# A Hymba layer on one core: the parts of the output weights are made at other turns and pinned on ScalarE

## The chip, the cores and the metric

The kernel runs on one core of one Trainium2 chip. The metric is the device time of one execution in microseconds; the median of three runs stands for a kernel. All data are float32. A core has five engines that run their own instruction streams and wait for each other by semaphores: TensorE (PE, with PEld for its weight loads), VectorE (DVE), ScalarE (ACT), GpSimd (POOL) and SyncE (SP), which here only issues transfers (DMA).

## The reference, cut to what matters

One decoder layer over 2048 tokens of width 1024. Half of the mixer is gated linear attention (GLA) with 4 heads in chunks of 64 tokens, half is dilated sliding-window attention with 8 heads and three (window, dilation) patterns. Both halves are put side by side and multiplied by W_out (1024 x 1024); the MLP follows.

```python
def reference(...):
    n = rmsnorm(x, attn_norm_g)
    # one projection W_in gives q, k, v, gates for GLA and q, k, v for attention
    mixed = concat([gla_mixer(...) * gate, combined dilated branches])
    h = x + mixed @ w_out
    h = h + square(relu(rmsnorm(h, mlp_norm_g) @ w_ff1)) @ w_ff2
    return rmsnorm(h, final_norm_g)
```

## The kernel before

The kernel runs in four stages. The input projection comes first. Then, up to about 880 us, attention and GLA run interleaved. The output projection (h = x + mixed @ W_out) goes to about 1080 us, and the MLP fills the rest.

Every large product works on numbers split in two: a high part, made by an ACT Copy to the type fp32r, and a low part, made by a DVE subtraction of the high part from the float32 value. Three matmuls, at L64, L65 and L66, then make one product (high by high, high by low, low by high). The split values of the mixer are `mT`: transposes at L393, the high part at L368 on ACT, the low part at L369 on DVE. The split values of W_out are `wo`, in eight blocks of 128 rows. For each, `load_wo` takes a buffer `woraw`, loads 512 KB into it (L985, issued by SP), makes the high part (L986, ACT) and the low part (L987, DVE). The projection of the first tokens needs all eight blocks.

Attention is cut into units of two or four blocks of 128 queries of one head and branch. A unit has three steps. `scores` makes the scores with two matmuls each (L744, L746) into the PSUM bank `ps_c`; DVE adds the bias and takes the row maximum (L756), and ACT takes the exponential into `pe` (L757). `transpose` transposes `pe` on PE (L766) into `ps_d`, and the result is copied to `pt` by ACT (L773) and DVE (L775) in turn. `values` multiplies `pt` by v (L785) into `ps_a`, and DVE copies that to O (L788). In turn k of the main loop stand the values of unit k - 2, the transposes of unit k and the scores of unit k + 3. There are four buffers each of `pe` and `pt`.

The GLA of 16 tiles of 128 tokens runs along, one step of a generator in most turns. Its instructions for tile t: the decay (matmul L912; exponentials L913 and L914 on ACT; products L915, L918 and L920 on POOL), the scores (matmul L925, masked copy L926 on DVE), the outputs (matmuls L945 and L946, copy L947, squares L949), the keys (transposes L955, copy L956), the output scale (the gate on POOL at L962, the scale on ACT at L964, and later the store to `mixD` at L862), and the state (matmul L970, DVE addition L973, ACT scale L975). The gates of the next tile but one are loaded to `sr` (L905), the values to `gv` (L904).

The branches of attention are combined on POOL and, for the last pair of heads, on DVE (the lines around L822 to L845).

What sets the order: the main loop records the instructions turn by turn, with a table `plan` of calls that a turn makes first (`at_unit`). From there a scheduler orders each engine's instructions by its own estimate of when they can start; `tc.keep_in_program_order(x)` pins x behind the instruction recorded just before it on its engine. SP issues its transfers strictly in its order, so a transfer that waits for its data holds up all those behind it. The eight calls of `load_wo` stand at turns NU - 28 + 3i for i = 0 to 7, so the last is 7 turns ahead of the end of the units. The load of x and of the mixer's tiles (`mx`, L1157) for the output projection follows behind all this, and the projection's first transposes (L393) are ordered into the last turns of attention.

Of the kernel before, what the change touches and what calls it, by code (L numbers as in the profile page):

```python
# [10 lines left out]
F32 = mybir.dt.float32  # L11
FR = mybir.dt.float32r
I32 = mybir.dt.int32
AF = mybir.ActivationFunctionType
OP = mybir.AluOpType
# [3 lines left out]
D = 1024  # L19
# [11 lines left out]
AHEAD, LAG = 3, 2  # L31
# [7 lines left out]
def emit(tc, a, stop=99):  # L39
    nc = tc.nc  # L40
    V, A, G, T, SP = nc.vector, nc.scalar, nc.gpsimd, nc.tensor, nc.sync
# [6 lines left out]
    def ps(tag):  # L48
        return psum.tile([128, 512], F32, name="ps_" + tag, tag=tag, bufs=BANKS[tag])

    def slot(name, dt=F32, n=SLOT):

        return up.tile([128, SLOT], dt, name=name, tag="u", bufs=25)[:, :n]

    def view(t, shape):
        n = int(np.prod(shape))
        names = "abcd"[:len(shape)]
        return t[:, :n].rearrange(f"p ({' '.join(names)}) -> p {' '.join(names)}", **dict(zip(names, shape)))
# [9 lines left out]
    def token_rows(ap, c, row, width=D):  # L68

        return bass.AP(tensor=ap.tensor, offset=ap.offset + c * 128 * row,  # L70
                       ap=[[row, 16], [16 * row, 8], [1, width]])
# [23 lines left out]
    def rstd_of(ssq, width, n=1, bias=eps):  # L95
        r = stat(n)
        A.activation(r, ssq, AF.Ln, bias=bias, scale=1.0 / width)
        A.activation(r, r, AF.Exp, scale=-0.5)
        return r
# [754 lines left out]
    def issue_later(n, *args):  # L854

        due.append((clock[0] + n, args))
# [37 lines left out]
    def gla_load(t):  # L894
        if t < NT:
            tk = slice(t * 128, t * 128 + 128)
            SP.dma_start(gst["g"][t % 2], glD[tk])
            SP.dma_start(gst["gq"][t % 2], gqD.rearrange("j p s -> p j s")[:, :, tk])
            SP.dma_start(gst["gk"][t % 2], gkD.rearrange("j p s -> p j s")[:, :, tk])

    def gla_load_v(t):
        if t < NT:
            tk = slice(t * 128, t * 128 + 128)
            SP.dma_start(gst["gv"][t % 2], gvD[tk])  # L904
            SP.dma_start(gst["sr"][t % 2], srD[tk])  # L905

    def gla_decay(t):

        g, ep, em = gst["g"][t % 2], gst["ep"][t % 2], gst["em"][t % 2]
        pb = view(ps("o"), (2, 256))  # L910
        for j in range(2):
            T.matmul(pb[:, j, :130], g[:, j * 128:j * 128 + 128], gst["rT"], start=True, stop=True)  # L912
        A.activation(ep, pb[:, :, :130], AF.Exp)  # L913
        A.activation(em, pb[:, :, :128], AF.Exp, scale=-1.0)  # L914
        G.tensor_tensor(em, em, gst["gk"][t % 2], op=OP.mult)  # L915
        for s in range(2):
            r = slice(64 * s, 64 * s + 64)
            G.tensor_tensor(gst["eq"][t % 2][r, :, s], ep[r, :, :128], gst["gq"][t % 2][r], op=OP.mult)  # L918
        if t:
            G.tensor_tensor(gst["w"][t % 2], gst["ep"][1 - t % 2][:, :, 129], ep[:, :, 128], op=OP.mult)  # L920

    def gla_scores(t):
        em, pa = gst["em"][t % 2], view(ps("o"), (4, 128))
        for j in range(2):
            T.matmul(pa[:, 2 * j:2 * j + 2], em[:, j], gst["eq"][t % 2][:, j], start=True, stop=True)  # L925
        V.copy_predicated(gst["AT"], gst["cm"][:, None, :].to_broadcast([128, 4, 128]), pa)  # L926

    def gla_steps():

        gla_decay(0)  # L930
        yield
        gla_scores(0)
        yield
        for t in range(NT):
            more = t + 1 < NT
            if more:
                gla_decay(t + 1)
                yield
            st, at, eq, em = gst["SS"], gst["AT"], gst["eq"][t % 2], gst["em"][t % 2]
            gv, sr, o, ss = gst["gv"][t % 2], gst["sr"][t % 2], gst["o"][t % 2], gst["ss"][t % 2]  # L940
            po = view(ps("o"), (2, 256))
            for j in range(2):
                for s in range(2):
                    h, oh = 2 * j + s, po[:, j, s * 128:s * 128 + 128]
                    T.matmul(oh, eq[:, j, s], st[:, j], start=True, stop=False)  # L945
                    T.matmul(oh, at[:, h], gv[:, h * 128:h * 128 + 128], start=False, stop=True)  # L946
            A.activation(o.rearrange("p (j s) e -> p j (s e)", s=2), po, AF.Copy)  # L947
            for h in range(4):
                A.activation(gst["sq"], o[:, h], AF.Square, accum_out=ss[:, h:h + 1])  # L949
            yield  # L950
            if more:
                kn = gst["kn"]
                pk = view(ps("o"), (2, 128))
                for j in range(2):
                    T.transpose(pk[:, j], em[:, j], ident)  # L955
                A.activation(kn, pk, AF.Copy)  # L956
                gla_load(t + 2)
                gla_load_v(t + 1)
                yield
                gla_scores(t + 1)  # L960
            rr = rstd_of(ss, 128, 4)
            G.tensor_tensor(o, o, view(sr, (4, 128)), op=OP.mult)  # L962
            for h in range(4):
                A.activation(o[:, h], o[:, h], AF.Copy, scale=rr[:, h:h + 1])  # L964
            issue_later(6, token_rows(mixD, t, D, width=512), o.rearrange("p h e -> p (h e)"))
            yield
            if more:
                pi, w = view(ps("o"), (2, 256)), gst["w"][1 - t % 2]
                for j in range(2):
                    T.matmul(pi[:, j], kn[:, j], gv[:, j * 256:j * 256 + 256], start=True, stop=True)  # L970
                for s in range(2):
                    r = slice(64 * s, 64 * s + 64)
                    V.tensor_tensor(st[r], st[r], pi[r, :, s * 128:s * 128 + 128], op=OP.add)  # L973
                for j in range(2):
                    A.activation(st[:, j], st[:, j], AF.Copy, scale=w[:, j:j + 1])  # L975
                yield

    wo = a["w_out"].rearrange("o (c p) n -> p (o c) n", p=128)
    WO = []

    def load_wo(n):
        for c in range(len(WO), len(WO) + n):
            raw = slot("woraw")[:, :D]
            w = view(slot("wo", FR), (2, D))
            SP.dma_start(raw, wo[:, c])  # L985
            A.activation(w[:, 0], raw, AF.Copy)  # L986
            V.tensor_tensor(w[:, 1], raw, w[:, 0].bitcast(F32), op=OP.subtract)  # L987
            WO.append(w)

    list(heads)  # L990
    for part in range(4):
# [32 lines left out]
    def at_unit(n, *f):  # L1024
        plan.setdefault(n, []).append(f)
# [45 lines left out]
    NU = len(units)  # L1071
    for i in range(8):
        at_unit(NU - 28 + 3 * i + AHEAD, load_wo, 1)
    gla = gla_steps()
    for k in range(-AHEAD, NU + LAG):
        tr, pv, sc = iter(()), iter(()), iter(())
# [354 lines left out]
    for at in range(7, len(jobs1)):  # L1431
# [13 lines left out]
        if at in (len(jobs1) - 4, len(jobs1) - 2):  # L1445
            n = (at + 4 - len(jobs1)) // 2
# [5 lines left out]
    for ph, (j, half) in enumerate(phases):  # L1452
        P = [bank() for _ in range(4)]
        for k in range(8):
            n = 8 * ph + k
# [53 lines left out]
def build(nc, inputs, stop=99):  # L1509
    arrays, aps = {}, {}  # L1510
    for name in _INS:
        arrays[name] = np.ascontiguousarray(inputs[name])
    arrays.update(_constants())
    for name, v in arrays.items():
        aps[name] = nc.dram_tensor(name, v.shape, mybir.dt.from_np(v.dtype), kind="ExternalInput").ap()
    aps["out"] = nc.dram_tensor("out", (1, S, D), F32, kind="ExternalOutput").ap()
    with tile.TileContext(nc, schedule_with_timeline_sim=True) as tc:
        emit(tc, aps, stop)
    return arrays
# [10 lines left out]
```

## Time and profile before

| what | us |
|---|---|
| median of 3 runs | 2313.16 (2312.07 to 2315.47) |
| the profiled execution | 2312.57 |
| its span | 2310.8 |
| PE busy | 2282.6 |
| DVE busy | 1550.3 |
| ACT busy | 1179.3 |
| POOL busy | 307.7 |

The mean granted clock of PE was 0.995 over the span. The page cuts the span in forty slices; attention and GLA end in slice 16 of them, where the output projection starts.

How to read it: a row of a view of waits names the instruction that waited and the one that released it, then the time in total, how often, and the longest. A row of a timeline gives the start in us from the span's start, the duration, the engine (SPq is SP's queue), the line, the operation, and the tiles out<-in; a run of like instructions is one row with its count, and in brackets stands the idle time before it, with what ended it. Rows of one engine overlap a little at their ends, so the distance of two starts is the time that an instruction holds its engine.

### The profile page before, as it was taken

How to read it: one execution, taken by the hardware profiler on the slowest of the kernel's cores; microseconds unless marked ns; L12 is line 12 of the kernel's file. 1: busy time of each engine (PE TensorE's matmuls, PEld its weight loads, DVE VectorE, ACT ScalarE, POOL GpSimd, SP SyncE). 2: the span in 40 equal slices, each digit the busy share in tenths (PEclk: the TensorE clock that was granted, in tenths of full speed). 3: DMA queues.
4: the chain of work that ended last, by engine and by line, in shares of the span. 5: the costliest groups of instructions: out<-in, count | busy, mean ns of one | idle time of the engine just before them, and what ended most of it. 6: DMA issues, size and time to landing. Idle time of an engine off the chain costs nothing.

```text
span 2310.8 us, 34890 instructions
## 1 busy us (share of the span) xinstructions
PE 2282.6 (99%) x12652; PEld 1975.6 (85%) x12652; DVE 1550.3 (67%) x2863; ACT 1179.3 (51%) x2368; POOL 307.7 (13%) x394
## 2 busy tenths in 40 slices
PE   8999999999999999999999999999999999999998
PEld 7977998799999998888888888888888888888887
DVE  8887778766667676346877788777755346447444
ACT  5574546435877873235555566555543323225224
POOL 1120002025385672000000000000000100000002
PEclk9999999999999999999999999999999999999999
DMA  4457854786668864678644447444486477447553
GB/s 165 144 183 230 250 161 125 215 254 229 209 203 249 253 218 143 210 244 279 208 153 151 151 163 265 151 151 150 150 278 238 155 280 251 148 166 279 188 170 109
DMA packets 341805, 457.59 MB, mean 198 GB/s; under 512 B 18118, under 2 KB 214231, under 8 KB 336257
## 3 DMA queue, kind: packets, MB, share of 16 engines
q1 hardware_dynamic: 336878, 446.71, 59.3%
q10 hardware_dynamic: 4754, 8.66, 1.0%
q8 instruction: 99, 1.62, 0.3%
q14 instruction: 74, 0.60, 0.1%
HBM read 292.99 MB, written 167.02 MB: 199 GB/s over the span
## 4 chain that ended last, share of the span: by engine, by line
PE 51%; ACT 1%; DMA 0%; DVE 0%; issue 0%; DVEq 0%; ACTq 0%
PE ps_c L64 6%; PE ps_c L65 6%; PE ps_c L66 6%; PE ps_a L65 4%; PE ps_a L66 4%; PE ps_d L65 4%; PE ps_d L64 4%; PE ps_a L64 4%; PE ps_d L66 4%; PE ps_o L65 2%; PE ps_o L66 2%; PE ps_o L64 2%; DMA w1raw<-w_ff 0%; ACT scr L1355 0%; DVE hb L369 0%; ACT hb L368 0%
## 5 line engine op out<-in xcount | busy, mean ns | idle before, releaser
L369 DVE TENSOR_TENSOR ca<-ra,ca 128x1024 fp32r<-128x1024 f32 x112 | 138.0, 1233 | 161.6 <-ACT ca L368 161.6
L368 ACT ACTIVATE ca<-ra 128x1024 fp32r<-128x1024 f32 x112 | 118.0, 1053 | 221.3 <-PE ps_c L66 184.3
L368 ACT ACTIVATE w1comb<-w1raw 128x512 fp32r<-128x512 f32 x224 | 140.0, 627 | 153.7 <-PE ps_c L66 55.7
L1357 POOL TENSOR_TENSOR suma<-suma,gs 128x512 f32<-128x512 f32 x16 | 23.4, 1475 | 1393.7 <-ACT scr L1355 1393.7
L369 DVE TENSOR_TENSOR w1comb<-w1raw,w1comb 128x512 fp32r<-128x512 f32 x224 | 153.9, 689 | 51.8 <-ACT w1comb L368 51.7
L785 PE MATMUL ps_a<-v,pt 128*128 128x65 f32 x1200 | 178.2, 252 | 2.5 <-ACT pt L773 1.8
L785 PEld LDWEIGHTS ps_a<-v,pt 128*128 128x128 f32 x1200 | 175.1, 195 | 3.5 <-ACT pt L773 2.1
L757 ACT ACTIVATE pe<-pe,O 128x256 f32<-128x256 f32 (+1 forms) x384 | 156.6, 453 | 39.4 <-DVE O L756 36.1
L766 PE MATMUL ps_d<-ident,pe 128*128 128x128 f32 x600 | 159.9, 279 | 0.0
L756 DVE CUSTOM_DVE_ANT_0 pe<-ps_c,nb 128x256 f32<-128x256 f32 (+1 forms) x384 | 126.9, 361 | 39.6 <-PE ps_d L766 18.4
L207 ACT ACTIVATE wcomb<-wraw 128x512 fp32r<-128x512 f32 (+2 forms) x126 | 97.2, 773 | 88.7 <-PE ps_o L65 22.6
L368 ACT ACTIVATE cb<-rb 128x1024 fp32r<-128x1024 f32 x56 | 59.4, 1060 | 159.3 <-PE ps_o L65 98.8
L66 PE MATMUL ps_c<-cb,ca 128*128 128x512 f32 x336 | 130.7, 389 | 0.0
L66 PE MATMUL ps_c<-hb,w1comb 128*128 128x512 f32 x336 | 130.7, 389 | 0.0
L65 PE MATMUL ps_c<-cb,ca 128*128 128x512 f32 x336 | 130.7, 389 | 0.0
L64 PE MATMUL ps_c<-hb,w1comb 128*128 128x512 f32 x336 | 130.7, 389 | 0.0
L65 PE MATMUL ps_c<-hb,w1comb 128*128 128x512 f32 x336 | 130.7, 389 | 0.0
L64 PE MATMUL ps_c<-cb,ca 128*128 128x512 f32 x336 | 130.7, 389 | 0.0
L766 PEld LDWEIGHTS ps_d<-ident,pe 128*128 128x128 f32 x600 | 110.1, 187 | 0.1
L369 DVE TENSOR_TENSOR cb<-rb,cb 128x1024 fp32r<-128x1024 f32 x56 | 68.3, 1222 | 62.0 <-ACT cb L368 62.0
L1219 ACT ACTIVATE acc<-acc 128x512 f32<-128x512 f32 x128 | 79.6, 631 | 51.5 <-DVE acc L1239 35.8
L64 PE MATMUL ps_a<-wo,mT 128*128 128x512 f32 x256 | 101.3, 396 | 0.0
(419 smaller groups left out, 7038.9 us busy)
## 6 DMA issues: line engine op xcount, KB each, us to landing
ra<-actD SPq DMA_DIRECT2D x56, 1024.0 KB, 6.9
actD<-acc SPq DMA_DIRECT2D x192, 256.0 KB, 2.3
rb<-w_ff SPq DMA_DIRECT2D x72, 512.0 KB, 4.8
w1raw<-w_ff SPq DMA_DIRECT2D x32, 1024.0 KB, 6.2
k<-kD SPq DMA_DIRECT2D x16, 1024.0 KB, 7.9
rb<-hTD SPq DMA_DIRECT2D x13, 1024.0 KB, 7.1
wraw<-w_in SPq DMA_DIRECT2D x48, 256.0 KB, 3.7
cmb<-boD SPq DMA_DIRECT2D x16, 528.0 KB, 7.0
```

The lines of the kernel that those rows point to most:

```text
L64: T.matmul(out, sh, mh, start=first, stop=False)
L65: T.matmul(out, sl, mh, start=False, stop=False)
L66: T.matmul(out, sh, ml, start=False, stop=last)
L207: A.activation(hi, src, AF.Copy, scale=sc)
L368: A.activation(hi, src, AF.Copy)
L369: V.tensor_tensor(lo, src, hi.bitcast(F32), op=OP.subtract)
L756: V.tensor_tensor_reduce(p, s, bias, scale=1.0, scalar=BIG, op0=OP.add, op1=OP.min, accum_out=nm)
L757: A.activation(p, p, AF.Exp, bias=nm, scale=-1.0)
L766: T.transpose(pb[:, i * 128:i * 128 + 128], src, ident)
L785: T.matmul(self.b.opsum[:, n % 4], self.pt[:, i * 128:i * 128 + 128], self.b.v[:, blk, cols], start=first, stop=last)
L1219: A.activation(v, v, AF.Relu)
L1357: G.tensor_tensor(C[0], C[0], gF[:, :512], op=OP.mult)
```

## The change

`load_wo` only loads and puts the buffer on a list. A new function, `split_wo`, takes the oldest buffer and makes both parts. For blocks 0 to 5 it is called in the turn of the load, right behind it; for blocks 6 and 7 two turns later. All eight ACT copies are pinned behind the instruction recorded just before them on ACT. No instruction is added or removed, and the buffers are taken in the same order.

```diff
+    raw_wo = []
+
     def load_wo(n):
-        for c in range(len(WO), len(WO) + n):
+        for c in range(len(WO) + len(raw_wo), len(WO) + len(raw_wo) + n):
             raw = slot("woraw")[:, :D]
-            w = view(slot("wo", FR), (2, D))
             SP.dma_start(raw, wo[:, c])
-            A.activation(w[:, 0], raw, AF.Copy)
-            V.tensor_tensor(w[:, 1], raw, w[:, 0].bitcast(F32), op=OP.subtract)
-            WO.append(w)
+            raw_wo.append(raw)
+
+    def split_wo():
+        raw, w = raw_wo.pop(0), view(slot("wo", FR), (2, D))
+        tc.keep_in_program_order(A.activation(w[:, 0], raw, AF.Copy))
+        V.tensor_tensor(w[:, 1], raw, w[:, 0].bitcast(F32), op=OP.subtract)
+        WO.append(w)
...
     for i in range(8):
         at_unit(NU - 28 + 3 * i + AHEAD, load_wo, 1)
+        at_unit(NU - 28 + 3 * i + (2 if i > 5 else 0) + AHEAD, split_wo)
```

The lines behind it move by 5 or 6: the load is L986 in the changed kernel, the high part L991, the low part L992, and the loads of `mx` L1163; the GLA and the units keep their lines. The order of instructions differs on every engine, between the third block's copy and the first tiles of the output projection.

The first place is ACT at the third and fourth block (counted from one). `O_9415` is the output of the last head pair's branch (128, 1), with which attention ends: a softmax into `pe` that names it belongs to the last units. Before:

```order
L956 ACTIVATE gla<-ps_o 128x256
L986 ACTIVATE wo<-woraw 128x1024
L98 ACTIVATE stats<-stats 128x4
L986 ACTIVATE wo<-woraw 128x1024
L773 ACTIVATE pt<-ps_d 128x512
L757 ACTIVATE pe<-pe,O_9415 128x128
L757 ACTIVATE pe<-pe,O_9415 128x256 x3
```

The same place of ACT in the changed kernel:

```order
L956 ACTIVATE gla<-ps_o 128x256
L98 ACTIVATE stats<-stats 128x4
L773 ACTIVATE pt<-ps_d 128x512
L975 ACTIVATE gla<-gla 128x128 x2
L964 ACTIVATE gla<-gla,stats 128x128 x4
L913 ACTIVATE gla<-ps_o 128x260
L914 ACTIVATE gla<-ps_o 128x256
L991 ACTIVATE wo<-woraw 128x1024 x2
L757 ACTIVATE pe<-pe,O_9415 128x128
L757 ACTIVATE pe<-pe,O_9415 128x256 x3
```

The two copies have moved behind the state, the output scale and the next decay of the recurrence (L975, L964, L913, L914), and these have moved ahead of the softmaxes of `O_9415`.

PE at the same place, before, from the masked scores of the recurrence on:

```order
L925 MATMUL ps_o<-gla 128x256 x2
L744 MATMUL ps_c<-k_8676,qs 128x256
L746 MATMUL ps_c<-k_8785,qs 128x256
L744 MATMUL ps_c<-k_8676,qs 128x256
L746 MATMUL ps_c<-k_8785,qs 128x256
L785 MATMUL ps_a<-v,pt 128x65 x4
L766 MATMUL ps_d<-ident,pe 128x128
```

And in the changed kernel, from the values ahead of the same masked scores on; three more pairs of L945 and L946 and the scores of `ps_c` follow, and then the first transpose (L766) of the last units:

```order
L785 MATMUL ps_a<-v,pt 128x65 x4
L925 MATMUL ps_o<-gla 128x256 x2
L785 MATMUL ps_a<-v,pt 128x65 x4
L970 MATMUL ps_o<-gla 128x256 x2
L912 MATMUL ps_o<-gla 128x130 x2
L945 MATMUL ps_o<-gla 128x128
L946 MATMUL ps_o<-gla 128x128
```

The state (L970), the decay (L912) and the outputs of the next tile (L945, L946) stand ahead of that transpose now; before they came behind some units of it.

SP at the end of attention, before, with the last two blocks' loads:

```order
L810 DMA cmb<-boD_1_103 128x8x132
L985 DMA woraw<-w_out 128x1024 x2
L1157 DMA mx<-mixD 128x512
L1157 DMA mx<-mixD 128x384
L862 DMA mixD<-gla 16x8x512
```

In the changed kernel:

```order
L810 DMA cmb<-boD_1_103 128x8x132
L986 DMA woraw<-w_out 128x1024
L862 DMA mixD<-gla 16x8x512
L986 DMA woraw<-w_out 128x1024
L1163 DMA mx<-mixD 128x512
L1163 DMA mx<-mixD 128x384
```

The last block's load stands behind the store of a GLA tile now. On ACT both of the last copies (L991 x2) stand directly ahead of the first high part of `mT` (L368), where before they were eight and four rows ahead of it, among the last softmaxes.

## The prediction

> **What bounds the kernel now.** I read the page first: the span and the busy time of the engines.
>
> ```profile
> span 2310.8 us, 34890 instructions
> PE 2282.6 (99%) x12652; PEld 1975.6 (85%) x12652; DVE 1550.3 (67%) x2863; ACT 1179.3 (51%) x2368; POOL 307.7 (13%) x394
> ```
>
> PE sets the end, so the change is worth what it adds to or takes from PE's idle time, or from its clock. The two programs stand in the same order on every engine except between about 836 and 895 us. There I asked for PE's waits (780 to 1100 us):
>
> ```profile
> PE ps_o L925 <- POOL gla L915: 1.9, 1, 1.9
> PE ps_a L785 <- ACT pt L773: 1.8, 1, 1.8
> PE ps_a L785 <- DVE pt L775: 0.7, 1, 0.7
> ```
>
> Three waits in two places. The windows of 2 us show what each drags behind it (columns: busy time of PE, PEld, DVE, ACT, POOL; granted PE clock; DMA share; GB/s):
>
> ```profile
> 840.00:842.00 2.00, 1.70 (x7) 1.54 (x8) 2.00 (x8) 2.00 (x7) 2.00 (x3) 0.77 0.00 0
> 842.00:844.00 2.00, 2.00 (x13) 2.00 (x11) 2.00 (x4) 0.25 (x1) 2.00 (x2) 0.50 0.76 221
> 844.00:846.00 2.00, 2.00 (x18) 2.00 (x18) 1.25 (x8) 0.82 (x2) 2.00 (x2) 0.87 0.93 303
> ...
> 870.00:872.00 2.00, 1.29 (x13) 1.10 (x12) 2.00 (x9) 1.88 (x5) 1.24 (x1) 0.95 0.84 268
> 872.00:874.00 2.00, 2.00 (x11) 2.00 (x12) 1.99 (x5) 1.05 (x3) 0.00 (x0) 0.50 0.97 276
> 874.00:876.00 2.00, 2.00 (x16) 2.00 (x16) 1.94 (x7) 1.29 (x3) 0.00 (x0) 0.69 0.94 363
> ```
>
> After each wait the clock falls to 0.50 for some 3.4 us. The clock's part is 2 us times what is missing to 1: 2 x (0.23 + 0.50 + 0.13) = 1.72 at the first place, 2 x (0.05 + 0.50 + 0.31) = 1.72 at the second. So place one costs 1.90 + 1.72 = 3.6 us, place two 1.84 + 0.70 + 1.72 = 4.3. More than 7.9 us is not to be won here.
>
> **The change, part by part.** No instruction is added or taken out: the same eight loads, ScalarE copies (L986) and VectorE subtractions (L987) stand elsewhere, and with them the recurrence (GLA) of the last tiles.
>
> *Place two goes: -4.3.* There ACT waits for block 7's load, copies block 8 next, and the pt copy that PE needs stands behind both:
>
> ```profile
> 865.30 1.06 ACT L986 ACTIVATE wo<-woraw 128x1024 fp32r<-128x1024 f32 x1 [1.99 <-DMA woraw<-w_out]
> 866.26 0.49 ACT L757 ACTIVATE pe<-pe,O 128x256 f32<-128x256 f32 x1
> ...
> 868.23 1.04 ACT L986 ACTIVATE wo<-woraw 128x1024 fp32r<-128x1024 f32 x1
> 869.17 0.57 ACT L773 ACTIVATE pt<-ps_d 128x512 f32<-128x512 f32 x1
> ```
>
> In the new order both copies stand behind the last of these pt copies, so nothing PE needs for attention waits for them. I credit all of it. What becomes late instead is the output projection (below).
>
> *Place one grows: +4.5.* Blocks 3 and 4 were copied at 835.9 and 838.5, ahead of the softmaxes (L757) of the last head's next units. Now their two copies stand together behind the recurrence: ACT holds L964, L913, L914, the two copies, and only then those L757, for which PE's transposes (L766) wait. POOL feeds L964, in an order that the change leaves alone up to there:
>
> ```profile
> 835.74 1.28 POOL L845 TENSOR_TENSOR O<-O,cmb 128x512 f32<-128x512 f32 x1
> 836.98 2.31 POOL L918 TENSOR_TENSOR gla<-gla 64x256 f32<-64x256 f32 x2
> 839.37 0.20 POOL L920 TENSOR_TENSOR gla<-gla 128x2 f32<-128x2 f32 x1
> 839.52 0.73 POOL L915 TENSOR_TENSOR gla<-gla 128x256 f32<-128x256 f32 x1
> 840.20 4.75 POOL L845 TENSOR_TENSOR O<-O,cmb 128x512 f32<-128x512 f32 x3
> 844.91 1.28 POOL L962 TENSOR_TENSOR gla<-gla 128x512 f32<-128x512 f32 x1
> ```
>
> POOL has no gap, so L962 again ends at 846.2. Its slowest forms may quicken when DVE is idler:
>
> ```profile
> 808.50 1.44 POOL L918 TENSOR_TENSOR gla<-gla 64x256 f32<-64x256 f32 x2 [1.27 <-ACT gla L913]
> ```
>
> That saves 0.9 us in L918; if the last of the L845, which take 1.6 us each, come near the 1.28 of the first, another 0.8 goes: 844.5 is the earliest. Then the loads. SP issues block 4's load behind the load of the next sr tile (L905), which waits for that same L962:
>
> ```profile
> 846.22 0.33 SPq L905 DMA_DIRECT2D gla<-srD  x1
> 846.67 0.36 SPq L985 DMA_DIRECT2D woraw<-w_out  x1
> ...
> DMA to landing us min/median/max: 4.3/5.2/6.0
> ```
>
> (The last line is that of the woraw tile.) So block 4 lands at 846.67 + 4.3 = 850.97 or, with the quicker POOL, at 849.3. Its copy takes 0.96 from start to start, the first L757 0.40, and the first L766 can begin at 850.7 to 852.4. Before it PE has, from 838.4 on, only eight L785 printed in two groups, L925, L970, L912, L945 with L946 and two scores:
>
> ```profile
> 847.45 1.03 PE L970 MATMUL ps_o<-gla 128*128 128x256 f32 x4
> 848.13 0.47 PE L744 MATMUL ps_c<-k,qs 128*128 128x256 f32 x1
> ...
> 850.89 0.61 PE L912 MATMUL ps_o<-gla 128*128 128x130 f32 x4
> 851.25 0.36 PE L744 MATMUL ps_c<-k,qs 128*128 128x256 f32 x1
> ...
> 879.22 1.00 PE L785 MATMUL ps_a<-v,pt 128*128 128x65 f32 x8
> ```
>
> By starts that is 0.68 for L970 and as much for L925, 0.36 for L912, about 1.8 for L785, some 1.8 for L945 and L946 (eight row pairs at 0.22), 0.5 for the scores: 5.7 us. From 838.4 to 850.7..852.4 are 12.3 to 14.0 us, so PE loses 6.6 to 8.3 there, idle time and slow clock together, against 3.6 before: +3.0 to +4.7. A second slow stretch of the clock after the restart would add to it. I take +4.5, near the upper end, since POOL's order is unchanged and DVE stays busy. VectorE's L926 and L973 and the low parts stand in this chain too, but end under the wait for the load. Below nothing it could come only if L962 ended by 841.5, which the POOL rows don't allow.
>
> *ACT is late afterwards: +1.9.* The held-up softmaxes make a queue on ACT.
>
> ```profile
> 846.20:857.40 11.20, 11.20 (x106) 11.10 (x106) 10.04 (x30) 10.36 (x26) 5.60 (x6) 1.00 0.92 279
> 857.40:871.50 14.10, 11.97 (x108) 11.29 (x107) 11.38 (x38) 11.77 (x36) 9.79 (x17) 1.00 0.85 254
> L757 ACT ACTIVATE pe<-pe,O 128x256 f32<-128x256 f32 x42 | 19.5, 500 | 2.8 <-DVE O L756 2.7
> ```
>
> ACT was busy 22.1 us of these 25.3 and PE 23.2: ACT can hardly catch up. Pricing the instructions of the new order by their starts here (L757 0.40, L773 0.47, L964 0.30, a block's copy 0.96), ACT has 20.4 us from the first tile's output after the hold-up (L947) to the pt copies of the last units, PE 17.7 up to the values that read them. The lag is between 0 (ACT ahead by its four pe buffers) and 2.6; I take 1.9, nearer the rows than the cover.
>
> *The output projection begins late: +4.8.* Block 8's load is now queued on SP behind the store of the last recurrence tile (L862), which waits for ACT's L964; before, blocks 7 and 8 were issued together ahead of it:
>
> ```profile
> 858.59 2.21 SPq L985 DMA_DIRECT2D woraw<-w_out  x2
> ...
> 867.99 0.52 SPq L862 DMA_DIRECT2D mixD<-gla  x1
> ```
>
> Call T the end of that L964. The load is issued at about T + 0.6 and lands 4.3 to 6.0 later. Block 8's copy stands on ACT ahead of the high parts of mT (L368), its low part on DVE ahead of the low parts (L369):
>
> ```profile
> L987 DVE TENSOR_TENSOR wo<-woraw,wo 128x1024 fp32r<-128x1024 f32 x8 | 11.6, 1445 | 3.0 <-DMA mx<-mixD 1.7 <-ACT wo L986 1.4
> 871.49 0.57 ACT L368 ACTIVATE mT<-ps_c 128x512 fp32r<-128x512 f32 x1
> 882.06 0.68 DVE L369 TENSOR_TENSOR mT<-ps_c,mT 128x512 fp32r<-128x512 f32 x1
> ```
>
> Copy 0.96, low part 1.45, mT 0.57 and 0.68, with 0.3 between them, is 4.0: the first projection matmul (L64) comes at T + 8.9 to T + 10.6. PE's attention work ends at about T + 4.3, and it has 1.9 us besides (transposes L393, a GLA output). PE idles 2.7 to 4.4 us less what the lag above already covers; I take 3.1, and a slow stretch of 1.7 as after both waits above: +4.8. It is nothing if ACT's last softmaxes are so late that block 8 has landed; at most 6.1.
>
> Sum: 4.5 - 4.3 + 1.9 + 4.8 = +6.9. The profiled execution took 2312.57 us, 0.6 under the median of 2313.16: 2312.57 + 6.9 = 2319.5, and by the median 2320.1. I say 2320.
>
> The page "TensorE: Matmul & The Clock Gate" of the Trainium skill (in "HAM oscillation — how this bites in real kernels") makes an abstract rule of "no PE-idle gaps >~3.4µs". The trace differs: 1.90 us of idle already brought 0.50. By the page the old waits would have cost their idle time alone, so that 2.5 is won at place two, 4.7 to 6.4 lost at place one (6.6 to 8.3 less 1.9), and the end costs 3.1: with the lag some 8 us instead of 6.9, an estimate, with the same sign.
>
> **The rivals.**
>
> *Both stalls vanish, faster.* The recurrence comes early and block 4's load lands before ACT gets there; 2312.57 - 7.9 = 2305 at best, 2308 if half of place one stays. For it: the two places are all that PE loses, and the order takes both copies out from before the softmaxes. It decides when L962 ends before 841.5, or SP lets block 4's load go ahead of L905. Against it stand the POOL rows. Chance 0.14.
>
> *The end is covered, no change.* Block 8 lands while the last softmaxes run: L64 starts on time, the lag hides there too, and only place one against place two is left: 2312.57 + 3.0..4.7 - 4.3, with a lag of 0 to 1.5: 2311 to 2315, say 2313. For it: 857 to 871 us gives ACT most of the time, so T and the end of attention may lie farther apart than 4.3. Chance 0.22.
>
> *Place two does not go either.* DVE, busy 21.4 us of the 25.3 above, gets the low parts, the softmax maxima and the combine in one bunch after the hold-up, and the pt copies on DVE (L775) come as late as the 0.70 of before, or worse: the 4.3 credited come back, less what the lag counts twice, 2322 to 2327. Chance 0.14, within slower. That the change fails to do what it says is part of this: parts two turns behind their loads still wait for the load if SP holds that back as well, as it does for block 8.
>
> **How the numbers follow.** My forecast, by its sum: 0.50, with its own range of 2315 to 2325 (place one 3.0, no lag and the end's idle at 2.7 with its clock below; all upper ends above). About 0.2% (4.6 us) is what a measurement of this kernel can tell from no change: under 2308.5 and over 2317.8. Of the forecast's 0.50 nearly all lies over 2317.8, with the third rival 0.64 in all; no change 0.22; faster 0.14. The range that leaves out 2 in 10 reaches from 2311, the low end of the covered case, to 2326.
>
> **What would show it.** Right: a wait of PE of 3 to 6 us at L766 (for ACT's L757) near 845 to 852, ACT's copy L991 before it waiting for woraw, clock 0.50 after it; no wait of L785 near 870; then a wait of L64 or L393 on block 8 or mT near 885 to 895. Wrong: block 4 landing before 846, L962 ending long before 846, PE's transposes running through 840 to 850, or no idle time ahead of the first L64. Then the sum loses 4.5 or 4.8 and the first or the second rival holds.

## The result, and the profile after

The changed kernel takes 2325.1 us in the median of 6 runs (2323.69 to 2326.99), the kernel before 2312.68 us (2312.07 to 2315.47, 6 runs): 12.4 us slower, ratio 1.0050 with a 95% interval of 1.0037 to 1.0063. The profiled execution of the changed kernel took 2325.71 us, its span is 2323.9 us, 13.1 more than before.

The waits of PE from 780 to 1120 us in the changed kernel, those of 0.7 us or more, stand here where the kernel before had the three rows of the prediction:

```profile
PE ps_d L393 <- POOL O L845: 3.4, 1, 3.4
PE ps_a L64 <- DVE O L788: 2.4, 1, 2.4
PE ps_o L945 <- ACT gla L914: 2.0, 1, 2.0
PE ps_d L766 <- ACT pe L757: 1.8, 1, 1.8
PE ps_a L785 <- DVE pt L775: 1.4, 1, 1.4
PE ps_o L912 <- PE ps_o L970: 1.0, 1, 1.0
PE ps_c L744 <- DVE O L756: 1.0, 1, 1.0
PE ps_a L785 <- ACT pt L773: 0.7, 1, 0.7
```

Three windows cut the stretch into place one, place two and the end of attention. The first number behind the length is PE's busy time, the one behind the five engines PE's granted clock. Before:

```profile
836.00:858.00 22.00, 20.10 (x170) 19.64 (x170) 19.26 (x58) 16.61 (x38) 15.65 (x15) 0.92 0.77 243
858.00:880.00 22.00, 19.45 (x166) 18.77 (x165) 19.27 (x61) 16.49 (x48) 12.29 (x24) 0.92 0.86 275
880.00:898.00 18.00, 18.00 (x94) 15.16 (x93) 14.07 (x31) 6.12 (x19) 8.36 (x10) 1.00 0.22 68
```

And in the changed kernel:

```profile
836.00:858.00 22.00, 16.02 (x117) 14.64 (x116) 12.54 (x38) 11.71 (x30) 13.65 (x15) 0.92 0.62 205
858.00:880.00 22.00, 21.29 (x199) 20.77 (x198) 17.35 (x68) 19.51 (x59) 4.17 (x11) 1.00 0.56 151
880.00:898.00 18.00, 10.52 (x54) 8.46 (x53) 17.81 (x31) 4.19 (x8) 17.53 (x24) 0.81 0.59 220
```

Idle time is the length less PE's busy time, the clock's part the length times what is missing to 1. Place one: 5.98 us idle against 1.90, with the same clock, +4.1. Place two: 0.71 against 2.55, and 1.76 of slow clock gone, -3.6. The end: 7.48 against none, and 3.4 of slow clock, +10.9. Together +11.4 of the 13.1. Where the other 1.7 us lie is not shown. Such sums hold to a few us: the span less these losses is 2302.8 us before and 2304.6 here, and lies between 2298.8 (e6) and 2306.2 (e12) in the profiled executions of all the runs below.

Place one follows the chain that was drawn. ACT in the changed kernel:

```profile
844.30 1.28 ACT L964 ACTIVATE gla<-gla,stats 128x128 f32<-128x128 f32 x4
...
846.02 1.05 ACT L991 ACTIVATE wo<-woraw 128x1024 fp32r<-128x1024 f32 x1
850.34 1.06 ACT L991 ACTIVATE wo<-woraw 128x1024 fp32r<-128x1024 f32 x1 [3.27 <-DMA woraw<-w_out]
851.30 1.88 ACT L757 ACTIVATE pe<-pe,O 128x128 f32<-128x128 f32 x5
```

SP in it:

```profile
844.30 0.33 SPq L905 DMA_DIRECT2D gla<-srD  x1
844.72 0.45 SPq L986 DMA_DIRECT2D woraw<-w_out  x1
```

And PE:

```profile
851.74 0.48 PE L766 MATMUL ps_d<-ident,pe 128*128 128x128 f32 x1 [1.82 <-ACT pe L757]
```

The end is not as it was drawn. DVE in the changed kernel, 882 to 888 us, and below it POOL:

```profile
882.72 1.39 DVE L843 TENSOR_TENSOR cmb<-cmb,small 128x512 f32<-128x512 f32 x1
884.03 2.06 DVE L992 TENSOR_TENSOR wo<-woraw,wo 128x1024 fp32r<-128x1024 f32 x1
886.01 1.53 DVE L845 TENSOR_TENSOR O<-O,cmb 128x512 f32<-128x512 f32 x1
887.46 0.42 DVE L788 COPY O<-ps_a 128x260 f32<-128x260 f32 x1
```

```profile
883.52 3.47 POOL L843 TENSOR_TENSOR cmb<-cmb,small 128x512 f32<-128x512 f32 x2
...
890.02 1.71 POOL L845 TENSOR_TENSOR O<-O,cmb 128x512 f32<-128x512 f32 x1
```

Neither engine waits in these rows. Both are full of the combine of the last head pair, and PE waits for them: L64 for L788, which stands behind block 7's low part (L992), and L393 for the last L845 of POOL. Before, POOL began this L843 at 865.61. The first combine instruction of this pair, L822 on DVE, began at 859.97 before and at 876.63 now.

### The profile page after: what moved, and what is told of

It reads as the page before. It is cut to its first block, busy times and chain, and to the rows that moved or that the text cites. A ratio compares the mean times of both kernels' runs of the same rounds, so it can differ in the third digit from the quotient of the medians.

```text
span 2323.9 us, 34895 instructions
## 1 busy us (share of the span) xinstructions
PE 2285.2 (98%) x12652; PEld 1976.4 (85%) x12652; DVE 1553.6 (67%) x2863; ACT 1179.6 (51%) x2368; POOL 306.4 (13%) x394
## 4 chain that ended last, share of the span: by engine, by line
PE 51%; ACT 1%; DMA 0%; DVE 0%; issue 0%; DVEq 0%; ACTq 0%
PE ps_c L64 6%; PE ps_c L65 6%; PE ps_c L66 6%; PE ps_a L65 4%; PE ps_a L66 4%; PE ps_d L64 4%; PE ps_d L65 4%; PE ps_a L64 4%; PE ps_d L66 4%; PE ps_o L64 2%; PE ps_o L65 2%; PE ps_o L66 2%; DMA w1raw<-w_ff 0%; ACT scr L1361 0%; DVE hb L369 0%; ACT hb L368 0%
## 5 line engine op out<-in xcount | busy, mean ns | idle before, releaser
L368 ACT ACTIVATE ca<-ra 128x1024 fp32r<-128x1024 f32 x112 | 117.9, 1053 | 226.3 <-PE ps_c L66 186.1
L368 ACT ACTIVATE w1comb<-w1raw 128x512 fp32r<-128x512 f32 x224 | 139.9, 627 | 154.6 <-PE ps_c L66 57.3
L785 PE MATMUL ps_a<-v,pt 128*128 128x65 f32 x1200 | 176.1, 251 | 2.1 <-DVE pt L775 1.4
L785 PEld LDWEIGHTS ps_a<-v,pt 128*128 128x128 f32 x1200 | 172.7, 193 | 3.1 <-DVE pt L775 1.6
L766 PE MATMUL ps_d<-ident,pe 128*128 128x128 f32 x600 | 159.2, 279 | 1.8 <-ACT pe L757 1.8
L756 DVE CUSTOM_DVE_ANT_0 pe<-ps_c,nb 128x256 f32<-128x256 f32 (+1 forms) x384 | 127.2, 361 | 41.8 <-PE ps_d L766 18.1
L368 ACT ACTIVATE cb<-rb 128x1024 fp32r<-128x1024 f32 x56 | 59.4, 1060 | 154.1 <-PE ps_o L65 116.0
L64 PE MATMUL ps_c<-hb,w1comb 128*128 128x512 f32 x336 | 130.7, 389 | 0.0
L64 PE MATMUL ps_c<-cb,ca 128*128 128x512 f32 x336 | 130.7, 389 | 0.0
L766 PEld LDWEIGHTS ps_d<-ident,pe 128*128 128x128 f32 x600 | 109.3, 186 | 2.1 <-ACT pe L757 2.0
L64 PE MATMUL ps_a<-wo,mT 128*128 128x512 f32 x256 | 101.7, 398 | 2.7 <-DVE O L788 2.4
```

The costliest lines, as they stand in the source:

```text
L64: T.matmul(out, sh, mh, start=first, stop=False)
L368: A.activation(hi, src, AF.Copy)
L756: V.tensor_tensor_reduce(p, s, bias, scale=1.0, scalar=BIG, op0=OP.add, op1=OP.min, accum_out=nm)
L766: T.transpose(pb[:, i * 128:i * 128 + 128], src, ident)
L785: T.matmul(self.b.opsum[:, n % 4], self.pt[:, i * 128:i * 128 + 128], self.b.v[:, blk, cols], start=first, stop=last)
```

## The experiments

The order of instructions in each program, written out for every engine, shows which edit moves what. The two turns' delay alone gives the order of before, row for row on all five engines. The pins of the third and the sixth block alone, with no other pin, give the order of the changed kernel, row for row. The third block's pin moves the recurrence ahead (place one). The sixth block's pin moves the combine: its first L822 stands behind the 23rd softmax maximum (L756) of the last branch on DVE before, behind the 31st in the changed kernel, the 32nd with the sixth pin alone, and the 23rd wherever the sixth pin is missing. The runs that take these apart follow; times are medians, with the kernel before on the same chip at 2313.0 to 2313.4.

### e1: the store of GLA tile 14 leaves SP

On SP of the changed kernel the four loads of the combine (L810) go out at 866.13, since the store of GLA tile 14 ahead of them waits until 865.51; before they went out at 852.02.

```diff
-            issue_later(6, token_rows(mixD, t, D, width=512), ...)
+            if t != 14:
+                issue_later(6, token_rows(mixD, t, D, width=512), ...)
+            else:
+                A.dma_start(token_rows(mixD, t, D, width=512), ...)
```

> The changed kernel with one edit: the store of GLA tile 14 to mixD is issued by ACT, which makes its data, and not by SP; the orders of PE, DVE and POOL stay as they are. Theory A: most of the 10 us that PE loses at the end of attention come from that store, since it waits on SP from about 849 to 865 us and holds the four loads of the last pair's combine (cmb) behind it, so that the combine starts some 13 us late on DVE and POOL. Then the cmb loads go out near 850, the L845 of POOL end before PE needs them, and the time falls by 5 to 8 us, to about 2317 to 2320. Theory B: the end's loss is block 8's load behind the next GLA store and its parts on ACT and DVE, as forecast; this edit leaves them alone, and the time stays within 1.5 us of 2325.

Measured: 2323.98 us (1.0048, 1.0033 to 1.0063). SP issued the combine's loads early, as theory A asks:

```profile
852.93 4.65 SPq L810 DMA_DIRECT2D cmb<-boD  x4
```

But DVE, with its order unchanged, began the combine where it had:

```profile
877.11 0.23 DVE L822 TENSOR_TENSOR small<-O,cmb 128x8 f32<-128x8 f32 x2
```

Theory A falls. The loads were late, and nobody waited for them.

### e2: block 8's load ahead of the last GLA store

```diff
-        at_unit(NU - 28 + 3 * i + AHEAD, load_wo, 1)
+        if i < 7:
+            at_unit(NU - 28 + 3 * i + AHEAD, load_wo, 2 if i == 6 else 1)
```

> The changed kernel with block 8's load issued in the turn of block 7's, so that it stands ahead of the last GLA store on SP; the combine's loads stay where they are, behind the store of tile 14. Theory A (combine late): the first copies come earlier, but PE still waits for POOL's L845, and the time stays at 2322 to 2326. Theory B (block 8 late): the end's loss falls by about 5 us, to some 2320.

Measured: 2324.53 us (1.0052, 1.0035 to 1.0068). Both last copies ran at 880.38 without a wait, and the end kept most of its loss: PE waited 3.1 us for L788 and 1.5 for L845, and was idle for 6.31 us of the last window, against 7.48. Theory B, the step of my forecast, is worth less than a microsecond by the medians. The combine is late, as theory A says here, but by e1 not through the store of tile 14. So a third theory was needed, C: the place of the combine in DVE's order, which the sixth pin sets.

### e3, e5, e6, e7: one pin, or all but one

```diff
-        tc.keep_in_program_order(A.activation(w[:, 0], raw, AF.Copy))
+        hi = A.activation(w[:, 0], raw, AF.Copy)
+        if len(WO) == 2:
+            tc.keep_in_program_order(hi)
```

This is e3, the third block alone. In e5 the condition is `len(WO) != 5`, in e6 `len(WO) == 5`, in e7 `len(WO) > 5`.

> The changed kernel with only the third block's copy pinned; the parts of the last two blocks still two turns late, the other seven copies free. Theory A: the third block's pin alone moves the recurrence ahead at 838 to 852 us, so PE loses 6 us more there than before, as in the changed kernel (waits of L912, L945, L744 and L766), and, since SP's order at the end is nearly that of the changed kernel, the end loses too: 2320 to 2326. Theory B: the loss is that of the pins and the delay of the last two blocks: 2311 to 2315.

> The changed kernel with every copy pinned but the sixth block's, and the delay of the last two. Theory C: the sixth block's pin moves the start of the last pair's combine on DVE (L822) from behind the 23rd softmax of the last units to behind the 31st, and its work on DVE and POOL then stands in the way of the output projection; without that pin L822 stands where it stood before, the waits of L64 for L788 and of L393 for L845 go, and the 10 us at the end shrink to 2 or less; place one keeps its loss of about 6, and the stall at 868 to 876 may come back: 2316 to 2320. Theory B: the end's loss is that of blocks 7 and 8, whose pins and delay stay: 2323 to 2326.

> The changed kernel with only the sixth block's copy pinned. Theory C: place one as before, no stall at 868 to 876 since the combine's burst has left it, and the late combine's loss of about 10 at the end: 2313 + 10 - 4, so 2317 to 2321. Theory B, by which pins and delay of the last two blocks make the end's loss: 2309 to 2314.

> The changed kernel with only the last two blocks' copies pinned, and their delay. The order differs from that of before by a dozen rows: block 8's copy behind the pt copies, the last GLA store ahead of block 8's load on SP. Theory C: no combine late and no hold-up at place one, so 2311 to 2314, whichever way the copy goes. Theory B: L64 comes late by 3 us or more, 2317 to 2320.

| run | pins | us | ratio | interval |
|---|---|---|---|---|
| e3 | third | 2319.18 | 1.0030 | 1.0019 to 1.0041 |
| e5 | all but the sixth | 2319.98 | 1.0027 | 1.0017 to 1.0038 |
| e6 | sixth | 2325.26 | 1.0058 | 1.0042 to 1.0075 |
| e7 | last two | 2314.32 | 1.0007 | 0.9997 to 1.0016 |

e7 shows that pins and delay of the last two blocks, the part that the change is named for, make no difference that can be told. The third pin costs some 6 us; its 2319.18 lies just under theory A's 2320 to 2326. Place one loses there as A says; at the end PE has 0.94 us idle and 3.4 of slow clock, behind a wait for a pt copy, and L64 and L393 don't wait. e7's 2314.32 is 0.3 above theory C's range and far from B's. Without the sixth pin the changed kernel loses 7.0 instead of 12.4 us, L64 and L393 don't wait at the end, and PE has no idle time from 880 to 898 us. The sixth pin alone costs 12.3, more than the 4 to 8 that I wrote down: its last window is worse than that of the changed kernel.

```profile
880.00:898.00 18.00, 8.84 (x36) 7.02 (x37) 17.01 (x31) 3.67 (x7) 16.50 (x23) 0.64 0.59 213
```

There L393 waits 5.2 us for the mixer's load, which stands behind the last GLA store and block 8's load on SP, and 5.2 for L845. So the two pins don't add: 6.2 and 12.3 alone, 12.4 together. In e5, moreover, a stall as long as that of place two is back, though ACT copies blocks 7 and 8 without a wait for their loads, at 868.56 and 877.49, and PE doesn't wait for ACT:

```profile
878.66 0.69 PE L785 MATMUL ps_a<-v,pt 128*128 128x65 f32 x2 [3.35 <-DVE pt L775]
```

### e4 and e8: what the stall of place two is

e4 takes away the late loads of blocks 7 and 8, with no pins:

```diff
-        at_unit(NU - 28 + 3 * i + AHEAD, load_wo, 1)
-        at_unit(NU - 28 + 3 * i + (2 if i > 5 else 0) + AHEAD, split_wo)
+        at_unit(NU - 28 + min(3 * i, 15) + AHEAD, load_wo, 1)
+        at_unit(NU - 28 + 3 * i + AHEAD, split_wo)
```

> No pins; the loads of blocks 7 and 8 are issued in the turn of block 6's, ahead of the combine's loads, and the parts are made in the turns of before. Place one keeps the order of before. If place two's stall came from the late loads of blocks 7 and 8, as its rows say, it goes: 4.3 us less than before, about 2308 to 2310. Rival: the combine's loads, now behind 1 MB more on SP, come some 3 us later and hold up the end of attention: 2312 to 2316.

e8 takes POOL out of the last pair's combine, in the kernel before:

```diff
-                running[pr, t0] = combine(pr, t0, n, got[pr, t0 // 8], V if pr == 3 and t0 % 8 else G)
+                running[pr, t0] = combine(pr, t0, n, got[pr, t0 // 8], V if pr == 3 else G)
```

> The kernel before with all of the last pair's combine on DVE (two of its four parts were on POOL). It tests what the stall at 868 to 876 before was. Theory D: DVE and POOL slow each other there (L825 took 1.00 us on DVE, while other L825 took 0.19, with POOL in L843 and L845), and the pt copy on DVE (L775) is late for that; with POOL out of it the short DVE instructions keep to 0.2 us and PE's loss of 4.3 there falls to 2 or less: 2309 to 2312. Rival: the stall is ACT's wait for block 7's load and its two copies, as I forecast; it stays, and DVE has some 4 us of work more: 2313 to 2318.

e4 measured 2314.56 us (1.0005, 0.9995 to 1.0014), no difference that can be told, and the rival's number. ACT makes both copies at 860.77 without a wait, and PE stalls all the same, behind DVE. In part that is a new delay, the rival's: DVE had waited 0.87 and 1.37 us for the combine's loads, which come later here.

```profile
873.44 0.44 PE L785 MATMUL ps_a<-v,pt 128*128 128x65 f32 x2 [2.42 <-DVE pt L775]
```

```profile
870.38 1.06 DVE L825 TENSOR_TENSOR small<-small,O 128x8 f32<-128x8 f32 x1
871.36 1.08 DVE L825 TENSOR_TENSOR small<-small,cmb 128x8 f32<-128x8 f32 x2
872.37 0.42 DVE L788 COPY O<-ps_a 128x260 f32<-128x260 f32 x1
872.71 0.68 DVE L775 COPY pt<-ps_d 128x512 f32<-128x512 f32 x1
```

```profile
870.38 1.04 POOL L843 TENSOR_TENSOR O<-O,small 128x512 f32<-128x512 f32 x1
871.38 2.05 POOL L843 TENSOR_TENSOR cmb<-cmb,small 128x512 f32<-128x512 f32 x2
```

The DVE instruction on 8 numbers a partition lasts as long as POOL's on 512 beside it, from the same start. With POOL out of it, e8 has the same DVE instruction at

```profile
866.90 0.16 DVE L825 TENSOR_TENSOR small<-small,O 128x8 f32<-128x8 f32 x1
```

e8 measured 2313.37 us (1.0004, 0.9994 to 1.0013), which lies in the rival's range and not in theory D's. In its profiled execution (2310.86 us) the clock never falls in the second window, and L785 waits 0.4 us for ACT, which still waits 1.67 for block 7. But L393 waits now, 0.7 us for a pt copy of DVE and 1.2 for the mixer's loads, and the idle time of the window is 2.34 us against 2.55 before. So the short rows of DVE come back as theory D says, what PE saves is the slow clock, 1.76 us, and nothing of it can be told in the medians.

### e9 and e12: the same on the changed kernel

e9 puts e8's edit into the changed kernel; e12 adds the last three GLA stores on ACT (`if t < 13` in place of e1's `if t != 14`).

> The changed kernel with all of the last pair's combine on DVE. Theory C with D: the 10 us that PE loses at 880 to 896 come from the late combine, and its two halves on DVE and POOL slow each other (L992 2.06 us, L831 and L823 above 1.2, POOL's L845 ending at 891.7). With POOL idle there, DVE's rows go back to their short times, PE's wait for POOL's L845 (3.4 us) goes, and the loss shrinks by 4 us or more: 2317 to 2321. Place one keeps its 6. Rival: DVE alone has more to do ahead of the low parts and of L369, and L64 waits as long as before or longer: 2324 to 2330.

> The run with the combine on DVE (changed kernel, e9), and in it the stores of the last three GLA tiles issued by ACT: the orders of PE, DVE and POOL are those of e9, and on SP the loads of blocks 7 and 8 and of mx are held by no store any more. It tells what of the 6 us that e9 still loses at the end comes from loads queued behind the last GLA store, the step of my forecast. Theory S (queue of SP): block 8 and mx land some 5 us earlier or more, PE's wait of L393 for mx (2.6 us) goes and the loss at the end falls to 3 or less: 2316 to 2318.5. Theory O (order on DVE and ACT): the low parts and the combine, which keep their places, set the time all the same, and it stays at 2320 to 2322.

e9 measured 2320.86 us (1.0031, 1.0019 to 1.0043), 4.2 less than the changed kernel, with the DVE rows from 880 us on at their short times (L992 at 1.21). Its last window:

```profile
880.00:898.00 18.00, 14.16 (x75) 11.85 (x75) 17.97 (x59) 5.48 (x10) 0.00 (x0) 0.91 0.63 225
```

That is 3.84 us idle and 1.6 of clock, where the changed kernel had 7.48 and 3.4: half of the end's loss went with POOL out of the combine. How much of this is that the two no longer slow each other, and how much that DVE makes an L845 in 0.68 us where POOL took 1.27 and 1.71, is not separated. Whether the other half comes from late transfers is asked by e12, which measured 2320.94 us (1.0034, 1.0022 to 1.0045). SP of e12 issues both last blocks early, and ACT copies both without a wait at 880.51, the same moment as e9's first copy:

```profile
858.06 9.94 SPq L989 DMA_DIRECT2D woraw<-w_out  x2
```

PE then no longer waits 2.6 us for the mixer's load, and waits instead

```profile
885.42 1.56 PE L785 MATMUL ps_a<-v,pt 128*128 128x65 f32 x8 [3.36 <-DVE pt L775]
```

for a pt copy that DVE makes at 884.69, in e9 at 884.60, behind the combine's L843. Transfers issued 9 us or more earlier changed nothing: theory O holds, the late combine on DVE sets the time.

### e10 and e11: towards a faster kernel

e10 joins e4 and e8. e11 moves the second half of the third pair's combine, which keeps POOL busy at place one, two turns ahead.

```diff
-                        combine_at(pr - 1, 8 * half, 8, first - 2 + 7 * half, [first + 4 + 7 * half + n for n in range(8)])
+                        combine_at(pr - 1, 8 * half, 8, first - 2 + (7 - (2 if pr == 3 else 0)) * half, [first + 4 + (7 - (2 if pr == 3 else 0)) * half + n for n in range(8)])
```

> No pins; the loads of blocks 7 and 8 in the turn of block 6's, and the last pair's combine all on DVE: both suspected causes of the stall at 868 to 876 are taken away at once. If they are all there was, PE loses less than 1 us there instead of 4.1, and the time is 2309 to 2311. Rival: DVE is the bound in that stretch with the combine added, 2312 to 2316.

> As the run before, and the combine of the third pair (on POOL) two turns earlier in its second half. Place one's stall of 3.4 us (L925 waits for POOL's L915, which stands behind L845 of that combine) should shrink if POOL is free earlier: 2306 to 2309. Rival: the combine then meets other GLA steps on POOL, and the stall only moves: 2310 to 2314.

e10 measured 2316.19 us (1.0009, 1.0000 to 1.0017): a miss, and 0.2 above the rival's range too. The combine's loads, now behind the two blocks, let DVE wait:

```profile
863.73 0.17 DVE L822 TENSOR_TENSOR small<-O,cmb 128x8 f32<-128x8 f32 x1 [2.37 <-DMA cmb<-boD]
```

e11 measured 2314.52 us (1.0005, 0.9996 to 1.0014). This is a miss too: L925's wait is gone from its trace and no wait of PE there exceeds 1.1 us, but the time is that of before within what can be told. No version here is faster than the kernel before.

## Why the prediction came out as it did

The time, 2325.1, lies in the range (2311 to 2326) and on the forecast's side, 5 us above the forecast of 2320. That it lies in the range, 0.9 under its end, is in part luck: the largest loss came by a way that the sum didn't have, and the lag of 1.9 us in the sum, which didn't come, made up for some of it.

**Place one, +4.5 forecast, +4.1 measured: right in its chain.** L766 began at 851.74, within 850.7 to 852.4. (The terms of PE's work there add up to 5.8 us, where I wrote 5.7; nothing hangs on it.) Two links were off and cancelled: POOL was done with L962 at 844.3 (its early bound was 844.5, I had taken 846.2), and the load took 5.6 us from its issue at 844.72 to the copy at 850.34, where I had taken the shortest of before, 4.3. The wait of 3 to 6 us that I had named as a sign, at L766, was 1.8: the idle time is spread over four waits (L912, L945, L744, L766). By e3 it is the third block's pin that does it; why that pin moves the recurrence was not followed into the scheduler. The size depends on where the slow clock falls. In e3 it is 0.50 from 847 to 850 us, ahead of the wait of L766, which takes it up, and the first window loses 5.9 us (4.14 idle); in the changed kernel it falls behind that wait, at 852 to 854, and the loss is 7.7 (5.98 idle).

**Place two, -4.3 forecast, -3.6 measured: near in size, half of the cause missed.** I read the stall from the ACT copies ahead of L773, and that wait of 1.84 us stands in the row. A second chain ends in the same place, and its rows stand in the trace of before, which I passed over:

```profile
866.39 1.34 DVE L987 TENSOR_TENSOR wo<-woraw,wo 128x1024 fp32r<-128x1024 f32 x1 [1.66 <-DMA mx<-mixD]
867.65 1.00 DVE L825 TENSOR_TENSOR small<-small,O 128x8 f32<-128x8 f32 x1
868.58 1.32 DVE L825 TENSOR_TENSOR small<-small,cmb 128x8 f32<-128x8 f32 x2
...
871.19 0.68 DVE L775 COPY pt<-ps_d 128x512 f32<-128x512 f32 x1
```

```profile
865.61 3.02 POOL L843 TENSOR_TENSOR cmb<-cmb,small 128x512 f32<-128x512 f32 x2
868.60 2.64 POOL L845 TENSOR_TENSOR O<-O,cmb 128x512 f32<-128x512 f32 x2
```

DVE makes block 7's low part as soon as ACT's copy of it is done, at 866.36, so the late load holds up DVE too; then come the slow rows of L825, and the pt copy behind them. Taking away one chain leaves the other. Without ACT's part PE waits 3.8 us (e4) and 3.35 (e5) for DVE; with block 8's copy alone moved behind that pt copy (e7) it waits 1.45 for ACT and 1.55 for DVE; without POOL (e8) the idle time is nearly that of before. The waits of L785 were short, 0.7 us from 858 to 880 in the changed kernel and 1.1 in e6, where the copy of block 7 and the combine had both left the place. My reading had the first and not the second.

**ACT late afterwards, +1.9 forecast, 0.7 at most measured.** PE was busy 21.29 of 22 us from 858 to 880, with one wait of 0.7 for a pt copy of ACT. ACT had done the softmaxes in time; the time lies near the lower bound, 0.

**The output projection late, +4.8 forecast, +10.9 measured: the step that failed.** I said that block 8's load behind the last GLA store, its copy and its low part hold up the first matmul. The load is behind that store, and the copy waited for it (1.42 us at 882.83), but e2 and e12 bring it ahead at a gain of less than 1 us and of none. The waits that I had named as signs came at L64 and L393, but for O, with 0.4 us for mT. What holds PE up is the combine of the last pair. I had followed the GLA, the softmaxes and the copies through the new order, and not the small instructions L822 to L845 on DVE and POOL. The sixth pin puts them 16.7 us later, into the projection's first matmuls; half of their price goes when POOL is taken out (e9), the rest stays with early transfers (e12), and with L822 at its old place PE has no idle time there (e5). The third rival named this bunch on DVE, with the combine in it and 2322 to 2327, but put it at place two; it came at the end.

By windows 4.1 - 3.6 + 10.9 = 11.4, for 4.5 - 4.3 + 1.9 + 4.8 = 6.9 in the forecast.

The page "SBUF — State Buffer" of the Trainium skill (in "SBUF: two separate sides") says that a DVE operation with two SBUF inputs and a POOL operation that reads SBUF take a shared port pair as an exclusive lock for the whole instruction. The rows agree: 1.06 us for L825 beside a POOL instruction of 1.04 in e4, 0.16 without one in e8.

## What to carry to other kernels

A pin on one instruction can move everything that the scheduler orders behind it, as two of the eight pins did here: write out the order of every engine and look for what moved that the edit doesn't name, the small instructions of a side chain too, and where they land. A wait in front of the instruction that PE needs is not yet the whole cause of a stall: ask which engine would be next if that wait went, and look there for rows that last several times their usual duration. A transfer that goes out late costs only what the order of its consumers lets it cost; where they stand late in their engines' orders, an earlier load buys nothing.

## What the runs showed of the hardware

The clock doesn't follow the length of a single wait. One wait of 1.90 us was followed by 0.50 in the kernel before; in e4 waits of 1.36 and 2.42 us within 8 us left it at 1.00:

```profile
858.00:880.00 22.00, 18.23 (x165) 17.09 (x164) 19.40 (x58) 16.20 (x48) 11.25 (x22) 1.00 0.88 261
```

Whether this is where the single runs of one kernel differ by some 5 us (2311.99 to 2316.6 for e4) was not tried.
